# A two-layer hybrid decoder on one core: layer 1's down-projection without GpSimd, and the FFN's three-tap convolution accumulated in PSUM

## The chip, the cores and the metric

The kernel runs on one core of a Trainium2 chip. The metric is the device time of one execution in microseconds; the kernel before has a median of 2337.42 us over 3 runs. TensorE (PE) multiplies matrices into PSUM; VectorE (DVE), ScalarE (ACT) and GpSimd (POOL) do the element work; SyncE (SP) issues the transfers between HBM and SBUF.

## The reference, cut to what matters

The input is a sequence of 1024 positions of width 1024 in fp32. Two layers each have a mixer (layer 0: differential attention beside spatial gating; layer 1: a conformer convolution of width 31) and then a gated FFN with a causal convolution of width 3 over the positions. A final RMS norm ends it. The change lies in the FFN:

```
def conv_ffn(h, w_up, dw_w, dw_b, w_down):
    hh = causal_dwconv(h @ w_up, dw_w, dw_b)      # 2 * 2816 channels, 3 taps
    a, gate = jnp.split(hh, 2, axis=-1)
    return (a * jax.nn.silu(gate)) @ w_down       # 2816 -> 1024
```

## The kernel before, in words

Every fp32 operand of a matmul is split into a rounded high part and the rest: ACT casts the high part (L142), and DVE or POOL subtracts it to get the low part (L146). A product is then three passes (high by high, high by low, low by high).

**Up-projection.** `pair_steps` walks over 22 channel blocks j. For each j a gate block and a value block (128 channels each, 1024 positions) come from seven products of a Strassen-like scheme on half-size operands, 84 matmuls in all, in layers 0 and 1. ACT copies or DVE adds (L718, L720, L723) bring the products from PSUM into `row` tiles in SBUF. `conv` then makes the three taps of a row: ACT writes tap 2 and the bias into a tile `y` (L681), and DVE adds taps 1 and 0 with two SCALAR_TENSOR_TENSOR instructions over 1024 positions that read the row and `y` and write `y` (L683). The gate's `y` goes through Silu on ACT (L725), and DVE multiplies value by gate (L729). In layer 1, `finish` forms sums of two j's on POOL and DVE (L553 to L557) for the next stage and stores them to HBM in `phs`.

**Layer 1's down-projection.** `down_pair_steps` is again a seven-product scheme, with `ORDER` 2, 1, 5, 3, 6, 7, 4. Each product runs over 11 hidden pairs jj; product and jj make a unit of 12 matmuls (L819), so 77 units. A unit needs a weight quarter or a combination of quarters (`weight`, L781 to L787: products 5, 3, 6, 7 and 4 use combinations), its split, an activation block `ph` from `phs` and its split. Before the change POOL splits the weights, and POOL and DVE share the combinations. Quarters of the weight are loaded a product ahead of use; L771 is a DVE copy of one element, from the split activation of the unit before into the place that the load fills, which keeps the load behind that split. Product 2 accumulates in two single PSUM banks (`sbank`) and one double bank (`bank2`); there is one `bank2` buffer in the program. At the end of each product DVE adds the PSUM banks into the residual `xr` (L826), and the final norm follows.

**Order.** A scheduler simulates the program and orders each engine's instructions; a `pin` (new in the change) puts an instruction behind the one traced before it on its engine. The SP queue and each engine work strictly in their order.

Of the kernel before, what the change touches and what calls it, by code (L numbers as in the profile page):

```python
# [10 lines left out]
F32 = mybir.dt.float32  # L11
# [3 lines left out]
AF = mybir.ActivationFunctionType  # L15
# [33 lines left out]
HH = HT // 2  # L49
SLOT = {1: 0, 7: 1, 2: 2, 4: 3, 5: 4, 6: 5, 3: 6}  # L50
# [8 lines left out]
def trunk_kernel(ctx: ExitStack, tc: tile.TileContext, x, norm_mix_g, norm_ffn_g, ab_w_in, ab_w_out,  # L59
# [3 lines left out]
    nc = tc.nc  # L63
    x_in = x[0]
# [35 lines left out]
    def s4(shape, dt=F32):  # L100
        return wk.tile(shape, dt, tag="s4", name="s4", bufs=S4)

    def run(steps):
        for f in steps:
            f()
# [546 lines left out]
    def pair_steps(l, hT, T, js, up_pool):  # L652
# [26 lines left out]
        def conv(r, ct):  # L679
            y = s4([P, S])  # L680
            nc.scalar.activation(out=y, in_=r[:, 2:], func=AF.Identity, scale=dw[:, 2, ct:ct + 1], bias=dw[:, 3, ct:ct + 1])  # L681
            for k in (1, 0):
                nc.vector.scalar_tensor_tensor(out=y, in0=r[:, k:k + S], scalar=dw[:, k, ct:ct + 1], in1=y,  # L683
                                               op0=ALU.mult, op1=ALU.add)
            return y

        def f(j):
# [36 lines left out]
            yg = conv(rg, HT + j)  # L724
            nc.scalar.activation(out=yg, in_=yg, func=AF.Silu)  # L725
            product(A, 4, a4, False, True)
            nc.scalar.copy(out=rv_[:, 2:2 + CH], in_=A)
            yv = conv(rv_, j)
            nc.vector.tensor_tensor(out=yv, in0=yv, in1=yg, op=ALU.mult)  # L729
# [15 lines left out]
    def down_pair_steps(l, dpool):  # L745
# [20 lines left out]
        def load(n, jj, after=None):  # L766

            k, h = QUARTER[n]
            dst, r = W[jj][k][:, h * 512:(h + 1) * 512], (k * HH + jj) * P
            if after is not None:  # L770
                nc.vector.tensor_copy(out=dst[:, 0:1], in_=after)  # L771
            nc.sync.dma_start(out=dst, in_=w_dn[r:r + P, h * 512:(h + 1) * 512])

        def weight(n, jj):
# [8 lines left out]
            if n == 3:  # L783
                nc.gpsimd.tensor_sub(out=b12, in0=b22, in1=b12)
                nc.vector.tensor_add(out=b11, in0=b11, in1=b12)
            if n == 7:
                nc.gpsimd.tensor_sub(out=b21, in0=b21, in1=b11)  # L787
# [7 lines left out]
        def f(n, js):  # L795
# [14 lines left out]
            for i, jj in enumerate(js):  # L810
                us.append((unit(weight(n, jj), "pool"), unit(raw[:, i, :], "dve")))
                if n in (2, 1, 5):
                    load({2: 1, 1: 5, 5: 3}[n], jj, us[-1][1][:, 1, 0:1].bitcast(F32))
# [307 lines left out]
    with tc.tile_pool(name="down", bufs=1) as dpool:  # L1121
# [5 lines left out]
        for c in range(NCH):  # L1127
            x_from(xd[1])(c)
        run(ds[4:k])
# [38 lines left out]
```

## Time and profile before

| what | value |
|---|---|
| median of 3 runs (lowest to highest) | 2337.42 us (2334.6 to 2345.59) |
| profiled execution, its time and its span | 2339.52 us, 2337.6 us |
| PE busy | 2158.9 us, 92% of the span |
| DVE, ACT, POOL busy | 72%, 48%, 51% |
| layer 0 up-projection | 686 to 997 us and a little beyond |
| layer 1 up-projection | 1799 to 2087 us |
| layer 1 down-projection | 2081 to 2326 us, its start overlapped with the above |

The profiled execution lies 2.1 us above the median. A share of busy time is an average; what an engine waits for within a stage is in the rows further below.

### The profile page before, as it was taken

What the parts mean: (1) busy time and instruction counts of PE and PEld (TensorE: products, weight loads), DVE (VectorE), ACT (ScalarE), POOL (GpSimd) and SP (SyncE); (2) the same over time, 40 slices, a digit from 0 to 9 for tenths busy, and PEclk for the clock granted to TensorE, in tenths of its full rate; (3) what the DMA queues carried; (4) which work ended last, traced back from release to release, by engine and by line L of the source; (5) the groups of instructions that cost most, each with busy time, mean ns of one, the idle gap of its engine ahead of it and who ended that gap; (6) DMA issues with size and microseconds to landing.
All of it is one profiled execution on the core that took longest, in us unless ns stands there. A gap on an engine that the chain in (4) does not pass through costs nothing.

```text
span 2337.6 us, 28662 instructions
## 1 busy us (share of the span) xinstructions
PE 2158.9 (92%) x9882; PEld 1763.6 (75%) x9882; DVE 1675.2 (72%) x2721; ACT 1120.9 (48%) x1971; POOL 1198.4 (51%) x923
## 2 busy tenths in 40 slices
PE   8888879899999999999999879889898999989797
PEld 6677768788788888878887658767687877777586
DVE  6675747963976666655699969995685677767876
ACT  4344535743444444543556564655443444444254
POOL 3312311222644444545589827972565555656954
PEclk9999979999999999999999979989999999999999
DMA  7736545536422222465533513422643222257333
GB/s 236 214 104 194 175 151 176 161 95 204 130 91 88 88 82 82 138 207 196 172 117 117 171 55 101 143 77 87 215 140 122 88 93 100 86 204 240 102 117 99
DMA packets 299953, 318.81 MB, mean 136 GB/s; under 512 B 12444, under 2 KB 221600, under 8 KB 299296
## 3 DMA queue, kind: packets, MB, share of 16 engines
q1 hardware_dynamic: 293920, 302.30, 40.6%
q0 software_dynamic: 5888, 14.68, 2.1%
q8 instruction: 78, 1.28, 0.2%
q14 instruction: 67, 0.55, 0.1%
HBM read 253.76 MB, written 63.18 MB: 136 GB/s over the span
## 4 chain that ended last, share of the span: by engine, by line
PE 58%; DVE 23%; issue 7%; POOL 5%; ACT 5%; DMA 2%; SPq 0%; ACTq 0%; POOLq 0%; DVEq 0%
PE bank L675 15%; PE bank L304 14%; PE bank L267 11%; PE bank L856 6%; PE bank L819 5%; DVE sbank L1004 5%; DVE s L683 3%; DVE hl L146 3%; POOL hl L146 2%; DVE y L180 1%; POOL ap L1001 1%; ACT s L681 1%; PE sbank L464 1%; PE sbank L819 1%; ACT hl L142 1%
## 5 line engine op out<-in xcount | busy, mean ns | idle before, releaser
L146 POOL TENSOR_TENSOR hl<-raw,hl 128x512 fp32r<-128x512 f32 x456 | 671.7, 1491 | 510.4 <-ACT hl L142 486.4
L304 PE MATMUL bank<-big,hl 128*128 128x512 f32 x2112 | 500.8, 396 | 8.8 <-DVE big L223 2.7
L304 PEld LDWEIGHTS bank<-big,hl 128*128 128x128 f32 x2112 | 398.7, 191 | 95.1 <-ACT big L222 4.9
L142 ACT CAST hl<-raw 128x512 fp32r<-128x512 f32 x616 | 357.6, 617 | 228.5 <-PE bank L856 64.5
L267 PE MATMUL bank<-hl,big 128*128 128x512 f32 x1728 | 428.5, 402 | 20.8 <-POOL hl L146 9.8
L267 PEld LDWEIGHTS bank<-hl,big 128*128 128x128 f32 x1728 | 326.8, 193 | 91.9 <-POOL hl L146 10.4
L675 PE MATMUL bank<-big,hl 128*128 128x512 f32 x1440 | 346.9, 392 | 9.6 <-DVE row L720 8.2
L675 PEld LDWEIGHTS bank<-big,hl 128*128 128x128 f32 x1440 | 270.2, 189 | 72.0 <-DVE row L720 11.5
L683 DVE SCALAR_TENSOR_TENSOR s<-row,dw,s 128x1024 f32<-128x1024 f32 x120 | 198.1, 1651 | 123.3 <-ACT s L681 106.7
L675 PE MATMUL bank<-t,hl 128*128 128x512 f32 x1080 | 266.7, 396 | 6.9 <-ACT hl L142 6.9
L1004 DVE SCALAR_TENSOR_TENSOR sbank<-yb,cw,sbank 128x512 f32<-128x512 f32 x352 | 248.0, 747 | 6.0 <-ACT sbank L993 3.2
L856 PE MATMUL bank<-hl 128*128 128x512 f32 x1056 | 247.7, 392 | 4.3 <-DVE hl L146 3.9
L675 PEld LDWEIGHTS bank<-t,hl 128*128 128x128 f32 x1080 | 204.2, 190 | 53.9 <-ACT hl L142 8.0
L146 DVE TENSOR_TENSOR hl<-raw,hl 128x512 fp32r<-128x512 f32 x160 | 170.9, 1088 | 90.3 <-ACT hl L142 90.1
L856 PEld LDWEIGHTS bank<-hl 128*128 128x128 f32 x1056 | 196.2, 188 | 51.3 <-DVE hl L146 11.0
L819 PE MATMUL bank<-hl 128*128 128x512 f32 x726 | 176.4, 394 | 3.1 <-DVE xr L826 2.3
L1001 POOL TENSOR_TENSOR ap<-ap,pr 128x512 f32<-128x512 f32 x112 | 154.0, 1375 | 35.3 <-ACT ap L996 21.4
L819 PEld LDWEIGHTS bank<-hl 128*128 128x128 f32 x726 | 137.7, 190 | 33.9 <-DVE xr L826 2.7
L142 ACT CAST hl<-s 128x512 fp32r<-128x512 f32 x101 | 62.7, 621 | 163.0 <-DVE s L698 87.5
L146 DVE TENSOR_TENSOR hl<-ph,hl 128x512 fp32r<-128x512 f32 x72 | 101.9, 1428 | 44.8 <-ACT hl L142 44.8
L577 DVE SCALAR_TENSOR_TENSOR s<-bank,dw,s 128x510 f32<-128x510 f32 x112 | 83.4, 745 | 50.4 <-ACT s L574 49.0
L1000 ACT ACTIVATE pr<-yb,cw 128x512 f32<-128x512 f32 x112 | 80.8, 723 | 72.4 <-POOL ap L1001 72.1
(209 smaller groups left out, 2666.1 us busy)
## 6 DMA issues: line engine op xcount, KB each, us to landing
raw<-in_ffn_w_up SPq DMA_DIRECT2D x116, 512.0 KB, 4.3
raw<-in_ffn_w_down SPq DMA_DIRECT2D x44, 512.0 KB, 3.9
raw<-phd SPq DMA_DIRECT2D x44, 512.0 KB, 4.7
ph<-phs SPq DMA_DIRECT2D x33, 512.0 KB, 4.5
raw<-in_ab_w_in SPq DMA_DIRECT2D x64, 256.0 KB, 3.4
raw<-in_conv_w_in SPq DMA_DIRECT2D x32, 512.0 KB, 4.1
qd<-s SPq DMA_DIRECT2D x32, 256.0 KB, 2.9
qk<-qd POOLq DMA_DIRECT2D x8, 1024.0 KB, 7.3
```

What stands on the lines that cost most here:

```text
L142: nc.scalar.copy(out=hl_hi, in_=raw)
L146: eng.tensor_sub(out=hl_lo, in0=raw, in1=hl_hi.bitcast(F32))
L267: nc.tensor.matmul(ps, lhsT=hT[c][:, sa, d, tok(t)], rhs=units[d][:, sw, :], start=(n == 0), stop=(n == 3 * DT - 1))
L304: nc.tensor.matmul(ps, lhsT=hv[d // 4][:, sw, d % 4, :], rhs=hT[:, sa, d, :], start=(n == 0), stop=(n == 3 * DT - 1))
L577: nc.vector.scalar_tensor_tensor(out=y[:, sh:], in0=ps[:, :CH - sh], scalar=dw[:, k, ct:ct + 1], in1=y[:, sh:], op0=ALU.mult, op1=ALU.add)
L675: nc.tensor.matmul(ps, lhsT=hv[:, sw, d, :], rhs=B[n](sa, d), start=(start and i == 0), stop=(i == 11), skip_group_check=True)
L683: nc.vector.scalar_tensor_tensor(out=y, in0=r[:, k:k + S], scalar=dw[:, k, ct:ct + 1], in1=y, op0=ALU.mult, op1=ALU.add)
L819: nc.tensor.matmul(ps[k], lhsT=a[:, sa, k * P:(k + 1) * P], rhs=w[:, sw, :], start=(n in (5, 2, 1) and js[0] == 0 and i == 0), stop=(end a ...
L856: nc.tensor.matmul(ps, lhsT=phs[i][:, sa, k * P:(k + 1) * P], rhs=wds[i][:, sw, :], start=(dp == 0 and n == 0), stop=(dp == DP - 1 and n = ...
L1000: nc.scalar.activation(out=pr, in_=ys[ct][:, k:k + CH], func=AF.Copy, scale=cw[:, ct, k:k + 1])
L1001: nc.gpsimd.tensor_add(out=st["ap"], in0=st["ap"], in1=pr)
L1004: nc.vector.scalar_tensor_tensor(out=st["acc"], in0=ys[ct][:, k:k + CH], scalar=cw[:, ct, k:k + 1], in1=st["acc"], op0=ALU.mult, op1=ALU.add)
```

## The change

In `conv` the accumulator `y` becomes `bank2`, the one double bank of PSUM; Silu and the multiplication read it there and write SBUF tiles. In `down_pair_steps` all splits and combinations go to DVE, with the combinations pinned; the addition of b11 and b12 moves from product 3 to product 6; the one-element copies go; the loads are pinned on SP in the order of use, 5 units ahead of it, in place of behind a split; and the second half of the residual is loaded after 9 steps and not after 4.

```
+AHEAD = 5
+    pin = tc.keep_in_program_order
...
         def conv(r, ct):
-            y = s4([P, S])
+            y = bank2()
...
-            yg = conv(rg, HT + j)
-            nc.scalar.activation(out=yg, in_=yg, func=AF.Silu)
+            yg = s4([P, S])
+            nc.scalar.activation(out=yg, in_=conv(rg, HT + j), func=AF.Silu)
...
-            yv = conv(rv_, j)
-            nc.vector.tensor_tensor(out=yv, in0=yv, in1=yg, op=ALU.mult)
+            yv = s4([P, S])
+            nc.vector.tensor_tensor(out=yv, in0=conv(rv_, j), in1=yg, op=ALU.mult)
...
-            if after is not None:
-                nc.vector.tensor_copy(out=dst[:, 0:1], in_=after)
-            nc.sync.dma_start(out=dst, in_=w_dn[r:r + P, h * 512:(h + 1) * 512])
+            pin(nc.sync.dma_start(out=dst, in_=w_dn[r:r + P, h * 512:(h + 1) * 512]))
...
             if n == 3:
-                nc.gpsimd.tensor_sub(out=b12, in0=b22, in1=b12)
-                nc.vector.tensor_add(out=b11, in0=b11, in1=b12)
+                pin(nc.vector.tensor_sub(out=b12, in0=b22, in1=b12))
+            if n == 6:
+                pin(nc.vector.tensor_add(out=b11, in0=b11, in1=b12))
             if n == 7:
-                nc.gpsimd.tensor_sub(out=b21, in0=b21, in1=b11)
+                pin(nc.vector.tensor_sub(out=b21, in0=b21, in1=b11))
...
-                us.append((unit(weight(n, jj), "pool"), unit(raw[:, i, :], "dve")))
-                if n in (2, 1, 5):
-                    load({2: 1, 1: 5, 5: 3}[n], jj, us[-1][1][:, 1, 0:1].bitcast(F32))
+                us.append((unit(weight(n, jj), "dve"), unit(raw[:, i, :], "dve")))
+                p = ORDER.index(n) * HH + jj + AHEAD
+                if p // HH in (1, 2, 3):
+                    load(ORDER[p // HH], p % HH)
...
-        for c in range(NCH):
-            x_from(xd[1])(c)
-        run(ds[4:k])
+        x_from(xd[1])(0)
+        run(ds[4:9])
+        x_from(xd[1])(1)
+        run(ds[9:k])
```

From the lines 65 on the changed kernel's numbers are 2 higher (L683 is L685, L729 is L731, L146 is L148, L819 is L821, L826 is L828; L785 is L786 and L787 is L788). Up to the last j of layer 1 the order is the same on every engine, with `bank2` in place of an SBUF tile.

First PE, at the passage from the last j's seventh product (`big` weights, L675) to the down stage. The first name is the PSUM bank written, `hl` are split operands, of which each pair stands for one unit. Before:

```order
L675 MATMUL bank_17442<-big_13043,hl_17362 128x512 x12
L819 MATMUL sbank_17484<-hl_17491,hl_17494 128x512 x3
L819 MATMUL sbank_17485<-hl_17491,hl_17494 128x512 x3
L819 MATMUL bank2_17483<-hl_17491,hl_17494 128x512 x6
L675 MATMUL bank_17372<-big_14364,hl_17365 128x512 x12
L819 MATMUL sbank_17484<-hl_17515,hl_17518 128x512 x3
L819 MATMUL sbank_17485<-hl_17515,hl_17518 128x512 x3
L819 MATMUL bank2_17483<-hl_17515,hl_17518 128x512 x6
```

After the change, up to the same last product of the last j:

```order
L821 MATMUL sbank_17544<-hl_17551,hl_17554 128x512 x3
L821 MATMUL sbank_17545<-hl_17551,hl_17554 128x512 x3
L821 MATMUL sbank_17544<-hl_17573,hl_17576 128x512 x3
L821 MATMUL sbank_17545<-hl_17573,hl_17576 128x512 x3
L677 MATMUL bank_17430<-big_14396,hl_17423 128x512 x12
```

Behind it stand 12 single matmuls of units three and four on the two `sbank`s, and from the last of them on it reads:

```order
L821 MATMUL sbank_17545<-hl_17623,hl_17626 128x512
L821 MATMUL bank2_17543<-hl_17551,hl_17554 128x512 x6
L821 MATMUL bank2_17543<-hl_17573,hl_17576 128x512 x6
L821 MATMUL bank2_17543<-hl_17581,hl_17584 128x512 x6
L821 MATMUL bank2_17543<-hl_17623,hl_17626 128x512 x6
```

The `bank2` halves of the first four units now stand together behind the `sbank` halves of all four; before, each unit had both halves in a row.

Second DVE, at the same passage: the two convolutions of the last j (`row` tiles), the splits of the first units, and the sum L557. Before:

```order
L683 SCALAR_TENSOR_TENSOR s4_17456<-row_17368,dw1_440,s4_17456 128x1024
L771 COPY wb_17523<-hl_17528 128x1
L146 TENSOR_TENSOR hl_17572<-early_17486,hl_17572 128x512
L771 COPY wb_17523<-hl_17572 128x1
L146 TENSOR_TENSOR hl_17581<-early_17486,hl_17581 128x512
L771 COPY wb_17523<-hl_17581 128x1
L683 SCALAR_TENSOR_TENSOR s4_17474<-row_17370,dw1_440,s4_17474 128x1024 x2
L729 TENSOR_TENSOR s4_17474<-s4_17474,s4_17456 128x1024
L557 TENSOR_TENSOR s2_17562<-s4_17474,sx_17558 128x512
```

After the change, from the same convolution:

```order
L685 SCALAR_TENSOR_TENSOR bank2_17515<-row_17426,dw1_440,bank2_17515 128x1024
L148 TENSOR_TENSOR hl_17623<-wb_17579,hl_17623 128x512
L148 TENSOR_TENSOR hl_17626<-early_17546,hl_17626 128x512
L685 SCALAR_TENSOR_TENSOR bank2_17534<-row_17428,dw1_440,bank2_17534 128x1024 x2
L731 TENSOR_TENSOR s4_17533<-bank2_17534,s4_17514 128x1024
L148 TENSOR_TENSOR hl_17630<-wb_17579,hl_17630 128x512
L559 TENSOR_TENSOR s2_17616<-s4_17533,sx_17612 128x512
L148 TENSOR_TENSOR hl_17633<-early_17546,hl_17633 128x512
```

DVE now also splits the weights (`wb`), and the last multiplication L731 reads the `bank2` buffer that the down stage's first product takes next.

Third DVE, where product 3 gives way to product 6 (`w0` and `wb` are weight quarters). Before, the additions L785 of product 6 stand among the splits of product 5, for instance:

```order
L785 TENSOR_TENSOR w0_17512<-w0_17512 128x512
L771 COPY wb_17523<-hl_18037 128x1
L146 TENSOR_TENSOR hl_18073<-ph_18066,hl_18073 128x512
L781 TENSOR_TENSOR s2_18160<-wb_17621 128x512
L771 COPY wb_17523<-hl_18073 128x1
```

After the change they stand in product 6:

```order
L828 TENSOR_TENSOR xr_17702<-sbank_18026,xr_17702 128x512
L828 TENSOR_TENSOR xr_17702<-sbank_18027,xr_17702 128x512
L828 TENSOR_TENSOR xr_17702<-bank2_18025,xr_17702 128x512 x2
L786 TENSOR_TENSOR w0_17548<-w0_17548 128x512
L148 TENSOR_TENSOR hl_18509<-w0_17548,hl_18509 128x512
L148 TENSOR_TENSOR hl_18512<-ph_18506,hl_18512 128x512
L786 TENSOR_TENSOR w0_17570<-w0_17570 128x512
```

Each unit of product 6 is now an addition, the cast of its result on ACT, and two splits, in a row, behind the four residual additions that close product 3.

## Rows read from the trace of the kernel before

**Rows 1.** The page's chain of waits: shares of the span by line.

```profile
PE bank L675 15%; PE bank L304 14%; PE bank L267 11%; PE bank L856 6%; PE bank L819 5%; DVE sbank L1004 5%; DVE s L683 3%; DVE hl L146 3%; POOL hl L146 2%; DVE y L180 1%; POOL ap L1001 1%; ACT s L681 1%; PE sbank L464 1%; PE sbank L819 1%; ACT hl L142 1%
```

**Rows 2.** Stretches: busy (count) of PE, PEld, DVE, ACT, POOL; PE clock; DMA.

```profile
686.00:997.00 311.00, 310.87 (x1364) 255.05 (x1364) 206.50 (x215) 154.02 (x232) 153.60 (x130) 1.00 0.30 96
1799.00:2078.00 279.00, 268.37 (x1139) 215.60 (x1140) 200.59 (x181) 128.26 (x192) 163.47 (x126) 0.98 0.31 100
2081.00:2111.00 30.00, 21.90 (x90) 17.69 (x89) 20.17 (x22) 12.12 (x20) 17.55 (x11) 0.89 0.84 290
2111.00:2141.00 30.00, 30.00 (x134) 24.83 (x133) 22.57 (x32) 12.44 (x23) 16.70 (x12) 1.00 0.69 234
...
2171.00:2201.00 30.00, 22.45 (x77) 15.89 (x77) 27.81 (x25) 5.10 (x10) 30.00 (x20) 0.89 0.37 115
2201.00:2231.00 30.00, 27.70 (x116) 22.70 (x116) 17.13 (x14) 11.91 (x22) 23.23 (x16) 0.94 0.33 97
```

**Rows 3.** PE's waits in layer 1's up-projection: total us, times, longest.

```profile
PE bank L675 <- DVE row L720: 8.2, 5, 2.2
PE bank L675 <- ACT hl L142: 6.9, 3, 6.0
```

**Rows 4.** Chain of waits in layer 1's up-projection: start, us, what.

```profile
1859.02 1.91 DVE s L683
...
1913.91 2.00 DVE s L683
...
1916.51 1.65 DVE s L683
1918.68 1.69 DVE s L729
...
1922.29 1.59 DVE s L683
...
2067.48 1.92 DVE s L683
```

**Rows 5.** Single lines: count, duration ns min/median/max, first and last start.

```profile
L683 DVE SCALAR_TENSOR_TENSOR s<-row,dw,s x120: 1274/1554/2308, 707.7 to 2093.7; 128x1024 f32<-128x1024 f32 x120
L1004 DVE SCALAR_TENSOR_TENSOR sbank<-yb,cw,sbank x352: 730/746/757, 1162.7 to 1570.1; 128x512 f32<-128x512 f32 x176
L826 DVE TENSOR_TENSOR xr<-bank,xr x22: 665/678/692, 2122.9 to 2326.8; 128x512 f32<-128x512 f32 x22
L785 DVE TENSOR_TENSOR wb<-wb x8: 1437/1745/1775, 2170.2 to 2197.1; 128x512 f32<-128x512 f32 x8
```

**Rows 6.** PE's waits from 2081 to 2327 us.

```profile
PE sbank L819 <- POOL hl L146: 9.8, 8, 3.7
PE sbank L819 <- ACT hl L142: 8.1, 1, 8.1
PE bank L819 <- DVE xr L826: 2.3, 1, 2.3
```

**Rows 7.** Timeline of PE: start, us, what, [idle before, releaser].

```profile
2083.91 2.88 PE L675 MATMUL bank<-big,hl 128*128 128x512 f32 x12
2086.63 1.52 PE L819 MATMUL sbank<-hl 128*128 128x512 f32 x6
...
2105.77 2.07 PE L819 MATMUL sbank<-hl 128*128 128x512 f32 x4 [8.10 <-ACT hl L142]
```

**Rows 8.** Timelines of DVE (first three) and ACT: start, us, what, [idle, releaser].

```profile
1861.45 1.72 DVE L683 SCALAR_TENSOR_TENSOR s<-row,dw,s 128x1024 f32<-128x1024 f32 x1
...
2091.57 0.69 DVE L146 TENSOR_TENSOR hl<-early,hl 128x512 fp32r<-128x512 f32 x1
...
2095.91 1.23 DVE L729 TENSOR_TENSOR s<-s,s 128x1024 f32<-128x1024 f32 x1
...
2089.78 1.06 ACT L725 ACTIVATE s<-s 128x1024 f32<-128x1024 f32 x1 [1.70 <-DVE s L683]
...
2091.88 0.60 ACT L142 CAST hl<-wb 128x512 fp32r<-128x512 f32 x1
```

More of the change, by code (lines that the diff above doesn't have):

```diff
@@ L764, in place, with load @@
                 W[jj] = [W["big"][:, i, :], W["big"][:, i + 1, :]]
-        def load(n, jj, after=None):
+        def load(n, jj):
             k, h = QUARTER[n]
             dst, r = W[jj][k][:, h * 512:(h + 1) * 512], (k * HH + jj) * P
-            if after is not None:
-                nc.vector.tensor_copy(out=dst[:, 0:1], in_=after)
-            nc.sync.dma_start(out=dst, in_=w_dn[r:r + P, h * 512:(h + 1) * 512])
+            pin(nc.sync.dma_start(out=dst, in_=w_dn[r:r + P, h * 512:(h + 1) * 512]))
         def weight(n, jj):
```

## The prediction

> **What bounds the kernel now.** I read the page's chain of waits first, then busy time by stretch, then in each stretch that the change touches PE's waits, and at last the chain and the timeline where PE waits. The chain ends mostly on PE: L675, the up-projection's matmuls, is its largest share, and L683, the taps that the change touches, has 3% [rows 1]. Busy time by stretch says where PE is not full [rows 2]. In layer 0's up-projection PE is busy 310.87 of 311.00 us at clock 1.00: nothing that DVE does there is worth time. In layer 1's it is busy 268.37 of 279.00 us. In the down stage the slices differ: 134 matmuls in 30 us from 2111 us, but 90 from 2081 us, 77 from 2171 us and 116 from 2201 us, at clocks of 0.89, 0.89 and 0.94. Full pace is one unit of 12 matmuls in 2.72 us, the distance of the two starts 2083.91 and 2086.63 [rows 7], so 0.2267 us a matmul and 132.3 in 30 us. The three slices lose 9.6, 12.5 and 3.7 us by that; another 4 us lies scattered over the rest.
>
> In layer 1's up-projection PE's waits name DVE's additions out of PSUM (8.2 us) and one cast at the entry (6.9) [rows 3]. The chain shows what makes those additions late: a loop through DVE, ACT and POOL. The same L683 comes back at 1859.02, and for the fifth time after that at 2067.48 [rows 4]: 208.46 us over five turns, 41.7 us for two j's. Their 168 matmuls need 38.1 us. PE loses 3.6 us a turn, 18 us in five; before the first turn it is fed.
>
> **The taps in PSUM.** L683 lasts 1274 ns at least, 1554 at the median and 2308 at most; the spread goes with GpSimd's work beside it. An instruction of the same kind whose accumulator is in PSUM, L1004, spans 730 to 757 ns over all its 352 executions, with GpSimd's taps running beside it; L826, which reads one operand from PSUM, 665 to 692 [rows 5]. L685 becomes such an instruction at twice the length. L1004's 747 ns are 214 ns plus 512 elements at 0.96 per ns (the pace that 746 and 1274 ns for 512 and 1024 elements agree with, within 7 ns); 1024 elements give 1.28 us, and L683's own undisturbed minimum is the same 1.27. The upper bound is two L1004, 1.49. I take 1.28, since nothing in the 352 rows ever rose.
>
> On the chain of one turn stand L683 with 1.91, 2.00, 1.65 and 1.59 us [rows 4], and one of 1.72 [rows 8], which the chain writes as issue. At 1.28 each they save 0.63, 0.72, 0.37, 0.31 and 0.44, 2.5 in all. L729 at 1.69 falls to 1.21 to 1.25 (two L826, or its own undisturbed 1.23 [rows 8]), 0.45. ACT writes PSUM instead of SBUF at four places; I allow 0.05 us each (unknown; 0.1 at most, from either sign), 0.2 against. The turn becomes 41.7 - 2.5 - 0.45 + 0.2 = 39.0 us, still above PE's 38.1. Five turns give 13.5 us; the last j, 0.5 more: **14 us**, between 5 (L685 at 1.49, when only the contended ones gain) and 18 (PE never waits). What the chain has besides, the contended SBUF operations L695 to L698 and the three sums on POOL, stays.
>
> [...]
>
> One buffer for all accumulators is the other side of the change. Each j now runs ACT tap, two taps on DVE, Silu, and then the same with the multiplication: 1.24 + 2.56 + 1.06 and 1.24 + 2.56 + 1.23, 9.9 us of holding in 19.5 us. The buffer adds a wait only where the previous reader (L725 on ACT, L729 on DVE) is not done when the next L681 could start. ACT does L725 ahead of the value row's L681 in its own order already [rows 8], and the work that covers the other handing over is the next j's products. I put it at nothing, with 1 us a turn as the bound, 5 us.
>
> Layer 0: nothing in PE's 311 us; its last conv, before the down stage, ends earlier by at most 2 us. I take 1.
>
> **The down stage, its first units.** Before, PE does four units at the passage and stands 8.10 us until 2105.77, for a cast of a `ph` block [rows 7, 6], then four matmuls take 2.07 us where full pace is 0.91: the 9.6 us of the first slice, at a mean clock of 0.89. After, the four units' `bank2` halves wait for the last conv. The last product of the last j ends at a time t (2086.6 before). Then follow the copy out, Silu, and taps of the value row: L681 to t + 4.3, two taps to t + 6.9, L731 to t + 8.15, from the durations above. PE has 12 `sbank` matmuls for that, 2.72 us: it stands 5.4 us, and about 2 us go to the lower clock behind it, 7.5 to 8. Behind that stand 24 matmuls, 5.4 us, in which the `ph` splits of the next units must come: L559 waits on POOL's sums until about t + 12 (three of 1.3 us) and DVE's splits behind it cost 0.69 each [rows 8], two a unit, while PE needs 2.72. The SP queue asks for the first residual half and three weights before the first `ph`; at 290 GB/s [rows 2] that lands before PE wants it by some 2 us. So 9.6 becomes 7.5 to 8: gain **2 us**, between -4 (`ph` late) and +4.
>
> **The middle of the stage.** PE waited 9.8 us in eight places for POOL's low parts [rows 6], in the slice where POOL was busy 30.00 of 30.00 us [rows 2] and L785 took 1.75 us beside it [rows 5]; clock and knock-on make it 12.5 + 2.8. After, GpSimd has nothing to do there, so each DVE operation takes its undisturbed 0.69 us (L146 at 2091.57 [rows 8]). A unit of products 5, 3 and 7 needs a combination and two splits, 2.07 us, less than PE's 2.72; products 2 and 1 need 1.38. In product 6 the addition, the cast on ACT and the splits follow each other: 0.69 + 0.62 + 0.05 or so for the two hand-overs + 0.69 + 0.69 = 2.74, if the cast is not covered, the one place near PE's pace; DVE's own back-to-back rate of 0.60 brings it to 2.57. Loads no longer wait for splits; five units ahead are 13.6 us, against some 4 us to land. The 15.3 us become 1: gain **14**, between 9 and 15. At the boundary of products 3 and 6 PE waited 2.3 us for L826 and lost 3.7 with the clock; now four L828 (2.7) and the first unit of product 6 stand there in a row, 2.25 to 2.8 us: gain 0.5 (-1 to 2). The final norm beside the last products now shares DVE with splits: -0.5 (-3 to 0).
>
> **The sum.** 14 + 1 + 2 + 14 + 0.5 - 0.5 = 31 us. From the profiled 2339.5 us that is 2308.5; the median is 2.1 us under the profiled execution, so 2306. The likeliest's own range is 2299 to 2314.
>
> **Rivals.**
> 1. Only half arrives. Either L685 takes 1.49 us or another link sets the loop (the three POOL sums, 3.9 us a turn, or the SBUF operations beside them), so layer 1's loop gives 5 and not 14; or the product 6 chain runs at 3.0 us, 11 x 0.28 = 3, and `ph` comes late by 4. Gain 14 to 22, 2316 to 2324. For it: the rest of the loop is untouched. Against: the rows of L1004.
> 2. No change to measure. The taps' gain is taken by the single buffer (5) and the front (-4 in place of +2), and the middle gives 9 where PE merely waits elsewhere: 5 - 5 - 4 + 9 = 5, so 2332.
> 3. Slower: DVE cannot carry the down stage. The point from which it decides is 2.72 / 3 = 0.907 us an operation. If splits into the rounded format kept the 1.4 us that they often take beside GpSimd, units with a combination would take 4.2 us and the 33 of products 5, 3 and 6 alone would lose 33 x 1.5 = 49 us: net of the 15 us won elsewhere and the 15 of old waits, 19 us slower, 2356. Against it: splits of 0.69 us in rows where POOL is idle [rows 8], and POOL has no work left there but three sums and the norm.
> 4. More arrives: PE never waits in layer 1's loop, front at its best: 37 us, 2300.
>
> **How the numbers follow.** Forecast 0.66, half 0.17, no change 0.07, slower 0.06, more 0.04. The range must leave out no more than 2 in 10: forecast, more, and most of half, 2296 to 2324. About 0.5%, 12 us, is what a measurement of this kernel can tell from no change; faster by more than that are forecast, half and more, 0.87, from which I take 0.02 for halves that fall short: 0.85. Same 0.09, slower 0.06.
>
> **What would show it.** L685 at 1.28 us with minimum and maximum close together; the turn in layer 1's loop at 39 us, still on DVE and ACT, and PE's waits there at some 5 us; PE's stand at the first units 5 to 6 us, now for L731 and not for a `ph` cast; no waits for POOL in the down stage, DVE at 0.6 to 0.7 us a split, and PE at 130 matmuls or more in 30 us from product 1 to product 7. Wrong would be a longer L685, PE waits on `hl` in product 6, or a `ph` or weight transfer as the releaser in the middle.

## The result, and the profile after

The changed kernel takes 2305.7 us (median of 4 runs, 2301.7 to 2310.99), the kernel before 2336.39 us beside it: a ratio of 0.9862, 95% interval 0.9829 to 0.9895, so 31 us faster. Forecast were 2306 us. The profiled execution has a span of 2303.9 us, 33.7 less than before; of that some 4 us lie ahead of layer 1's up-projection (its matmuls resume after the entry wait at 1795.33 us and not 1799.31), 3.0 of them before layer 0's up-projection begins, where nothing was changed. The sum came out right, but not all of its terms did: that it fits to a microsecond is luck, as the part on the prediction shows.

Stretches of the changed kernel, columns as in [rows 2]: layer 0's up-projection, layer 1's, then six of the slices of 30 us from the passage to the down stage on.

```profile
682.70:993.70 311.00, 310.87 (x1366) 255.16 (x1365) 184.49 (x215) 154.24 (x233) 129.86 (x130) 1.00 0.30 96
1836.00:2042.00 206.00, 206.00 (x905) 169.52 (x904) 144.86 (x145) 99.23 (x147) 107.09 (x99) 1.00 0.31 102
...
2054.00:2084.00 30.00, 25.10 (x99) 19.41 (x99) 20.87 (x26) 13.43 (x20) 3.79 (x3) 0.89 0.61 217
2084.00:2114.00 30.00, 30.00 (x134) 24.86 (x133) 19.63 (x32) 12.47 (x22) 0.00 (x0) 1.00 1.03 390
...
2144.00:2174.00 30.00, 29.45 (x130) 24.09 (x129) 20.55 (x34) 12.44 (x22) 0.00 (x0) 1.00 0.40 119
2174.00:2204.00 30.00, 26.59 (x104) 21.04 (x103) 17.11 (x27) 7.98 (x14) 0.00 (x0) 0.89 0.28 86
...
2234.00:2264.00 30.00, 28.06 (x123) 22.59 (x122) 27.46 (x73) 18.22 (x35) 3.43 (x3) 1.00 0.52 167
```

Layer 0 was full and is full. Layer 1's loop, which had lost PE time in every turn, is now full too: 206.00 of 206.00 us. In the down stage three slices lose against 132.3 matmuls: the passage 7.5 us (99), the boundary of products 3 and 6 6.4 us (104), product 7 with the final norm 2.1 us (123). The middle of the stage is full but for 0.5 us (130 of 132.3), with GpSimd at nothing.

What PE waits for in the changed kernel from 2054 us on, the three largest: total us, times, longest.

```profile
PE bank L821 <- DVE s L731: 4.4, 1, 4.4
PE bank L821 <- ACT hl L144: 3.8, 3, 2.6
PE bank L821 <- DVE v L173: 1.5, 1, 1.5
```

No wait for GpSimd is left [rows 6]; the wait for a `ph` cast at the passage has become one for the last multiplication, as forecast.

### The profile page after: what moved, and what is told of

Same layout as the page of the kernel before. It is cut to its first block, busy times and chain, and to the rows that moved or that the text cites. A ratio compares the mean times of both kernels' runs of the same rounds, so it can differ in the third digit from the quotient of the medians.

```text
span 2303.9 us, 28559 instructions
## 1 busy us (share of the span) xinstructions
PE 2147.5 (93%) x9882; PEld 1760.4 (76%) x9882; DVE 1601.8 (70%) x2787; ACT 1120.9 (49%) x1971; POOL 1002.2 (43%) x824
## 3 DMA queue, kind: packets, MB, share of 16 engines
q8 instruction: 78, 1.28, 0.2%
## 4 chain that ended last, share of the span: by engine, by line
PE 70%; DVE 18%; issue 4%; DMA 3%; ACT 3%; POOL 3%; SPq 0%; ACTq 0%; DVEq 0%; POOLq 0%
PE bank L677 25%; PE bank L306 14%; PE bank L269 11%; PE bank L821 7%; PE bank L858 6%; DVE sbank L1006 5%; DVE hl L148 2%; PE sbank L821 2%; DVE y L182 1%; POOL ap L1003 1%; PE sbank L466 1%; POOL hl L148 1%; DVE xn L197 1%; PE sbank L213 1%; ACT hl L144 1%
## 5 line engine op out<-in xcount | busy, mean ns | idle before, releaser
L148 POOL TENSOR_TENSOR hl<-raw,hl 128x512 fp32r<-128x512 f32 x456 | 632.0, 1404 | 506.4 <-ACT hl L144 479.5
L685 DVE SCALAR_TENSOR_TENSOR bank<-row,dw,bank 128x1024 f32<-128x1024 f32 x120 | 154.5, 1287 | 140.6 <-ACT bank L683 138.1
L148 DVE TENSOR_TENSOR hl<-raw,hl 128x512 fp32r<-128x512 f32 x160 | 169.6, 1080 | 93.1 <-ACT hl L144 92.8
L821 PE MATMUL bank<-hl 128*128 128x512 f32 x726 | 176.8, 398 | 10.4 <-DVE s L731 4.4
L821 PEld LDWEIGHTS bank<-hl 128*128 128x128 f32 x726 | 139.4, 193 | 42.3 <-issue 5.8
L1003 POOL TENSOR_TENSOR ap<-ap,pr 128x512 f32<-128x512 f32 x112 | 153.8, 1373 | 34.5 <-ACT ap L998 20.7
L1112 POOL TENSOR_TENSOR xr<-xr,gain 128x512 f32<-128x512 f32 x10 | 14.5, 1479 | 202.3 <-ACT xn L1104 176.8
```

The source lines that it names most:

```text
L148: eng.tensor_sub(out=hl_lo, in0=raw, in1=hl_hi.bitcast(F32))
L821: nc.tensor.matmul(ps[k], lhsT=a[:, sa, k * P:(k + 1) * P], rhs=w[:, sw, :], start=(n in (5, 2, 1) and js[0] == 0 and i == 0), stop=(end a ...
L1003: nc.gpsimd.tensor_add(out=st["ap"], in0=st["ap"], in1=pr)
```

## The experiments

All times are medians with the kernel before run on the same chip. To see where a difference lies I read two lengths from each trace: "up", from where layer 1's up-projection resumes after its entry wait to the start of the last j's last matmul, and "down", from there to the start of the last matmul of the down stage. What follows, 13 to 14 us, is alike in all.

| kernel | us | before | ratio | 95% interval | up | down |
|---|---|---|---|---|---|---|
| before | | 2336.39 | | | 287.1 | 238.0 |
| changed | 2305.7 | 2336.39 | 0.9862 | 0.9829 to 0.9895 | 269.7 | 225.7 |
| e1 convolution only | 2319.93 | 2344.42 | 0.9898 | 0.9885 to 0.9912 | 268.3 | 237.8 |
| e2 down stage only | 2325.03 | 2344.42 | 0.9926 | 0.9913 to 0.9939 | 287.1 | 222.5 |
| e3 second tap to SBUF | 2303.45 | 2344.42 | 0.9829 | 0.9815 to 0.9842 | 271.1 | 219.8 |
| e4 weight splits on GpSimd | 2319.91 | 2344.42 | 0.9899 | 0.9884 to 0.9914 | 271.1 | 236.7 |
| e5 three additions ahead | 2302.3 | 2338.3 | 0.9848 | 0.9829 to 0.9866 | 271.0 | 218.8 |
| e6 last convolution in SBUF | 2309.57 | 2338.3 | 0.9875 | 0.986 to 0.989 | 271.2 | 223.3 |
| e7 norm off GpSimd | 2305.71 | 2338.3 | 0.9862 | 0.9848 to 0.9877 | 270.9 | 223.1 |
| e8 all three | 2303.64 | 2338.3 | 0.9851 | 0.9835 to 0.9868 | 271.1 | 220.2 |
| e9 e5 + e6, second half later | 2297.99 | 2339.83 | 0.9831 | 0.9813 to 0.9848 | 270.9 | 216.4 |
| e10 residual halves together | 2312.72 | 2339.83 | 0.9889 | 0.9872 to 0.9905 | 270.7 | 227.6 |
| e11 e3 + e5 | 2300.59 | 2339.83 | 0.9835 | 0.982 to 0.9851 | 271.1 | 217.1 |
| e12 changed, again | 2306.99 | 2339.83 | 0.9865 | 0.9847 to 0.9884 | 270.8 | 225.3 |

"Down" split by product, in us: the first column runs from the start of the last j's last matmul to the end of product 2, the others from the start of a product's first matmul to that of the next product's. Full pace is 29.9 us a product. Products 1 and 4, the second and the last, take 29.7 to 29.9 in every run.

| kernel | end of 2 | 5 | 3 | 6 | 7 |
|---|---|---|---|---|---|
| before | 37.3 | 45.4 | 34.1 | 29.9 | 31.6 |
| changed | 35.2 | 29.9 | 34.7 | 33.8 | 32.6 |
| e12 changed, again | 36.0 | 29.9 | 34.7 | 32.9 | 32.1 |
| e1 | 36.2 | 46.3 | 34.2 | 29.9 | 31.6 |
| e2 | 35.6 | 29.9 | 34.7 | 32.0 | 30.6 |
| e3 | 33.0 | 29.9 | 34.7 | 31.9 | 30.6 |
| e4 | 36.1 | 30.1 | 34.9 | 36.6 | 39.5 |
| e5 | 34.2 | 29.9 | 30.8 | 31.5 | 32.9 |
| e6 | 36.4 | 29.9 | 34.7 | 32.0 | 30.6 |
| e7 | 36.0 | 29.9 | 34.7 | 32.9 | 30.0 |
| e8 | 38.4 | 29.9 | 30.8 | 31.5 | 30.0 |
| e9 | 32.6 | 29.9 | 30.8 | 31.5 | 32.0 |
| e10 | 35.9 | 29.9 | 34.7 | 32.9 | 34.5 |
| e11 | 33.2 | 29.9 | 30.8 | 31.5 | 32.0 |

The two traces of one and the same changed kernel differ by 0.8 to 0.9 us in two of the columns; differences of that size mean nothing.

**The two halves apart.** e1 is the kernel before with the three edits of `conv`, Silu and the multiplication; e2 is the changed kernel with those three undone.

> The convolution in PSUM alone; the down stage as before. Theory (each half pays in its own stage): layer 1's up-projection, from its first matmul after the entry wait to the end of the last j's last product, takes 270 us as in the changed kernel (287.5 before), PE has no wait on DVE additions there, and the total gain over before is 17 to 20 us, less what the bank2 wait costs at the passage: the old down stage keeps its waits for GpSimd's low parts (about 10 us). So 2317 to 2321. Rival (the two halves need each other, since the old down stage takes bank2 for its first unit too): the first units stand 4 to 8 us longer than before and 2322 to 2328 remains. A turn of two j's is 38 to 39 us in both.

> The down stage without GpSimd and with loads in order alone; the convolution accumulates in SBUF as before. Theory: a turn of two j's stays at 41.7 us and L685's counterpart at 1.27 to 2.31 us; the down stage from the end of the last product to the last matmul takes 225 to 227 us (238 before, 226 with both), or some 3 less since bank2 is free at its start: the total is 2320 to 2326. Rival (GpSimd leaving the stage is worth nothing without the shorter passage): 2332 or more.

Each half pays in its own stage: e1's up is short and its down is that of before, e2 the other way round. (In e1 half a unit stands ahead of the last j's last product and not a whole one, which takes 1.4 us from its up and adds them to its down.) The stand that e1's rival expected at the first units is not there: they end no later than before. In e1 the old down stage meets the slice that it had before [rows 2], with GpSimd busy without a gap:

```profile
2147.00:2177.00 30.00, 22.09 (x73) 15.54 (x71) 29.13 (x25) 5.70 (x10) 30.00 (x19) 0.83 0.42 131
```

By these lengths the halves add up but for 3 us: e2's down is 222.5, the changed kernel's 225.7. (By the medians they gain 24.5 and 19.4 us on a chip whose kernel before is 5 to 8 us slower than elsewhere and on which the changed kernel wasn't run; the sum can't be read from those.) The 3 us are not a price of `bank2` at the passage: at the end of product 2 the two are level, 35.6 and 35.2 us, and the difference lies in products 6 and 7, to which the part on the final norm returns. With the accumulators in SBUF, e2 has a wait of 5.2 us at the passage for a cast instead, as the kernel before had [rows 7]:

```profile
2106.25 1.22 PE L821 MATMUL sbank<-hl 128*128 128x512 f32 x2 [5.19 <-ACT hl L144]
```

**Which operand makes a tap long.** In e3 the second tap reads PSUM and writes SBUF:

```
             y = bank2()
...
+            z = s4([P, S])
             for k in (1, 0):
-                nc.vector.scalar_tensor_tensor(out=y, in0=r[:, k:k + S], scalar=..., in1=y, ...)
+                nc.vector.scalar_tensor_tensor(out=y if k else z, in0=r[:, k:k + S], scalar=..., in1=y, ...)
-            return y
+            return z
```

Silu and the multiplication then work on `z` in SBUF.

> As the changed kernel, but the second tap reads the accumulator in PSUM and writes an SBUF tile, which Silu and the multiplication read. Theory (a second SBUF input is what GpSimd's work lengthens, the place of the output is not): both taps stay at 1.27 to 1.30 us, all 120 of them; the multiplication, which again reads two SBUF tiles, goes back to 1.2 to 1.7 us; the time stays within 3 us of the changed kernel, 2303 to 2309, as PE is the bound in the loop. Rival (an accumulator kept in PSUM on both sides is needed): half of the taps go to 1.6 us in the mean with a maximum over 2 us, the turn goes up by about 1 us, and the time to 2309 to 2314.

The taps of the changed kernel, of e3 (L686, one row for each output) and e3's multiplication: count, ns min/median/max, first and last start. First the changed kernel:

```profile
L685 DVE SCALAR_TENSOR_TENSOR bank<-row,dw,bank x120: 1277/1290/1292, 704.6 to 2070.9; 128x1024 f32<-128x1024 f32 x120
```

and e3:

```profile
L686 DVE SCALAR_TENSOR_TENSOR bank<-row,dw,bank x60: 1278/1289/1291, 707.0 to 2073.9; 128x1024 f32<-128x1024 f32 x60
L686 DVE SCALAR_TENSOR_TENSOR s<-row,dw,bank x60: 1268/1280/1282, 708.3 to 2075.2; 128x1024 f32<-128x1024 f32 x60
L732 DVE TENSOR_TENSOR s<-s,s x30: 1212/1220/2308, 716.5 to 2076.5; 128x1024 f32<-128x1024 f32 x30
```

With GpSimd at work beside them, e3's taps take 1278 to 1291 ns with their output in PSUM and 1268 to 1282 ns with it in SBUF: where the output goes makes 10 ns here at most. One input in PSUM was enough to keep every tap under 1.3 us, and the multiplication, which reads two SBUF tiles again, has its 2308 ns maximum back, against 1282 ns at most for the taps that write SBUF. e3 also hands `bank2` over one multiplication earlier: PE waits 2.9 us at the passage and not 4.4. Down is 219.8 us, 5.4 to 5.9 shorter than in the changed kernel's two profiles, of which the passage gives 2.2 to 3.0 and products 6 and 7 the rest. The median is 2 us below the changed kernel's, within what was expected. By the ratio, 0.9829, e3 would be the faster, but its interval overlaps with the changed kernel's, and it is from the chip with the slow kernel before: e11, which has e3's edit and one more that shortens down by another 2.7 us, has 0.9835 on another chip. That e3 beats the changed kernel is not shown by the times.

**GpSimd's place in the down stage.** e4 gives the weights' splits back, with the combinations on DVE and the loads in order:

```
-                us.append((unit(weight(n, jj), "dve"), unit(raw[:, i, :], "dve")))
+                us.append((unit(weight(n, jj), "pool"), unit(raw[:, i, :], "dve")))
```

> As the changed kernel, but the weights' low parts in the down stage are again subtracted on GpSimd; combinations stay on DVE and loads in program order. Theory (GpSimd's presence in the stage makes the waits): DVE's splits and combinations rise from 0.69 to 1.2 to 1.75 us while GpSimd splits, each low part on GpSimd takes 1.3 to 2.2 us, and in products 5, 3 and 6 a unit costs more than 2.72 us: PE waits for low parts return, 8 to 15 us in all, total 2312 to 2322. Rival (the loads in order were the gain, DVE's room is not needed): the time stays at 2304 to 2308 and PE waits for GpSimd are under 3 us.

The time is as the theory has it, 11 us of the down stage's gain gone, but not the place. Slices of e4:

```profile
2118.00:2148.00 30.00, 30.00 (x135) 24.82 (x134) 26.14 (x26) 13.27 (x25) 17.24 (x13) 1.00 0.57 193
2148.00:2178.00 30.00, 29.41 (x129) 23.67 (x127) 20.45 (x19) 11.50 (x22) 14.92 (x11) 1.00 0.43 132
...
2238.00:2268.00 30.00, 23.26 (x92) 17.77 (x91) 29.67 (x61) 16.77 (x35) 20.72 (x13) 0.94 0.42 133
```

Products 5 and 3 keep PE full although GpSimd splits and DVE's `ph` splits take 1.37 us beside it. What is lost lies in products 6 and 7. In product 6 a unit's addition, casts and splits follow each other; two additions stand 3.23 us apart, over PE's 2.72:

```profile
2198.69 0.68 DVE L786 TENSOR_TENSOR w<-w 128x512 f32<-128x512 f32 x1
2200.65 1.34 DVE L148 TENSOR_TENSOR hl<-ph,hl 128x512 fp32r<-128x512 f32 x1 [1.28 <-ACT hl L144]
2201.92 0.68 DVE L786 TENSOR_TENSOR w<-w 128x512 f32<-128x512 f32 x1
```

In the changed kernel they stand 2.66 us apart (2192.76, 2195.41, 2198.07). In the slice of product 7 PE loses 9.1 us, where GpSimd does splits and the norm's multiplications at once.

**The boundary of products 3 and 6.** The changed kernel loses 6.4 us there. PE first, then DVE:

```profile
2190.44 1.67 PE L821 MATMUL bank<-hl 128*128 128x512 f32 x6 [0.79 <-DVE xr L828]
2194.74 9.53 PE L821 MATMUL bank<-hl 128*128 128x512 f32 x28 [2.63 <-ACT hl L144]
```

```profile
2192.15 0.69 DVE L828 TENSOR_TENSOR xr<-bank,xr 128x512 f32<-128x512 f32 x1 [1.76 <-PE bank L821]
2192.76 0.68 DVE L786 TENSOR_TENSOR w<-w 128x512 f32<-128x512 f32 x1
2194.20 0.69 DVE L148 TENSOR_TENSOR hl<-w,hl 128x512 fp32r<-128x512 f32 x1 [0.76 <-ACT hl L144]
```

The fourth residual addition waits for product 3's last matmul, and product 6's first addition stands behind it in DVE's queue, though its operands have long been there. e5 makes the first three ahead:

```
-            if n == 6:
+            if n == 6 and jj > 2:
                 pin(nc.vector.tensor_add(out=b11, in0=b11, in1=b12))
...
+            if n == 3 and end:
+                for jj in (0, 1, 2):
+                    b11, b12 = W[jj][0][:, :512], W[jj][0][:, 512:]
+                    pin(nc.vector.tensor_add(out=b11, in0=b11, in1=b12))
```

> As the changed kernel, but product 6's first three additions of b11 and b12 (jj 0 to 2) are made at the end of product 3, ahead of the residual additions. Theory (the stand at the boundary of products 3 and 6 is the chain of L828, addition, cast and split behind the residual additions): PE's wait of 2.6 us for ACT's cast goes, the stretch of 30 us that holds the boundary gets back some 5 of the 6.4 us that it loses (104 matmuls before), and the down stage is 4 to 5 us shorter; the ratio to the kernel before is 0.002 lower. Rival (PE waits there for the residual additions to free banks, or the additions only move the wait into product 3's last units): the loss stays above 4 us.

The slice that holds the boundary is full in e5:

```profile
2176.00:2206.00 30.00, 30.00 (x135) 24.82 (x134) 20.59 (x33) 10.28 (x18) 0.00 (x0) 1.00 0.31 94
```

Down is 218.8 us, 6.4 to 6.9 under the changed kernel's two profiles; products 3 and 6 together lose 6.2 us less than in the first of them. The measured ratio is 0.0014 lower, within the intervals: the gain is seen in the trace. The longest wait in product 7 grew from 1.5 to 2.5 us.

**The passage.** e6 frees `bank2` before the down stage:

```
-        def conv(r, ct):
-            y = bank2()
+        def conv(r, ct, y):
...
+            last = l == 1 and j == js[-1]
-            nc.scalar.activation(out=yg, in_=conv(rg, HT + j), func=AF.Silu)
+            nc.scalar.activation(out=yg, in_=conv(rg, HT + j, yg if last else bank2()), func=AF.Silu)
...
-            nc.vector.tensor_tensor(out=yv, in0=conv(rv_, j), in1=yg, op=ALU.mult)
+            nc.vector.tensor_tensor(out=yv, in0=conv(rv_, j, yv if last else bank2()), in1=yg, op=ALU.mult)
```

> As the changed kernel, but the last j of layer 1 accumulates its two convolutions in SBUF tiles, so that bank2 is free when the down stage begins. Theory (the 4.4 us wait at the first units is for bank2 alone): no wait for the last multiplication is left, PE goes on through the first four or five units, then stands at most 2 to 3 us for a ph cast or a weight; the first units are 3 to 6 us shorter. Rival (the ph and weight transfers are as late as in the kernel before, bank2 only covers it): PE stands 4 to 8 us for a cast of a ph block instead and nothing is won.

The theory fell here: the wait for the multiplication is gone and a longer one stands in its place. PE, SP's queue and the chain of waits of e6, in this order:

```profile
2085.70 1.22 PE L821 MATMUL sbank<-hl 128*128 128x512 f32 x2 [7.16 <-ACT hl L144]
```

```profile
2073.85 0.38 SPq L869 DMA_DIRECT2D xr<-xd  x1
2075.05 0.33 SPq L809 DMA_DIRECT2D ph<-phs  x1
```

```profile
2075.42 9.01 DMA wb<-in_ffn_w_down
```

The scheduler, with its order changed, put the 2 MB of the residual's second half ahead of the first `ph` and its weight, which then took 9.0 us to land: it is this weight's cast that PE waits for. e6's down is still 2.4 us shorter than the changed kernel's first, but that is in products 6 and 7; its passage is no shorter (36.4 us to the end of product 2), as the rival has it. e9 tells this from a `ph` that is late by its own issue: it pins that load behind the loads traced before it (and has e5's additions).

```
-            nc.sync.dma_start(out=xr[c], in_=src[c * CH:(c + 1) * CH, :].rearrange(...))
+            i = nc.sync.dma_start(out=xr[c], in_=src[c * CH:(c + 1) * CH, :].rearrange(...))
+            if src is xd[1] and c == 1:
+                pin(i)
```

> As the changed kernel with the last j's convolutions in SBUF and three additions ahead, and with the load of the residual's second half pinned on SP behind the loads traced before it, so that it isn't put ahead of the first ph block. Theory (in the run with the last convolution in SBUF alone, the 7.2 us stand was for that 2 MB transfer ahead of the first ph block, whose own issue waits for the last tap): the first ph and its weight land 4 to 5 us after issue, PE stands 2 to 4 us at the sixth unit, and the passage is 3 to 5 us shorter than in the changed kernel; the ratio to the kernel before is 0.980 to 0.984. Rival (the first ph block is late by its own issue, which waits for the last tap, whatever stands ahead of it): PE still stands 5 us or more, and the ratio is that of the run with three additions ahead alone, 0.985.

In e9 the same weight lands in 5.0 us and PE stands 3.4 us. First the chain of waits, from the last tap on, then PE:

```profile
2074.14 1.21 DVE s L684
...
2075.40 0.33 SPq L809
...
2075.77 4.96 DMA wb<-in_ffn_w_down
```

```profile
2081.99 1.22 PE L825 MATMUL sbank<-hl 128*128 128x512 f32 x2 [3.40 <-ACT hl L144]
```

The passage is 2.6 to 3.4 us shorter than in the changed kernel's two profiles. So both were true in part: 3.8 us of the 7.2 were the 2 MB ahead, 3.4 us remain because the first `ph` is asked for only once the last tap is done (2075.40), and the weight stands behind it in SP's queue. That the `ph` tile lies where a `row` tile lay would explain why it is asked for so late; it was not tried.

**The final norm.** e7 has `eng = nc.vector` for all of L1112.

> As the changed kernel, but the final norm's multiplications by the gain (L1112) are on VectorE and not on GpSimd. Theory (the splits of 1.78 us around 2231 to 2237 us are long because GpSimd multiplies beside them): no split in the down stage is over 0.8 us, PE's wait of 1.5 us and its loss of 2.1 us in product 7 fall to under 1, and the time is 1 to 3 us lower. Rival (the waits there come from the norm's small instructions in DVE's queue): the wait in product 7 stays or grows by the ten multiplications of 0.69 us, and the time is the same or up to 3 us higher.

In the changed kernel, GpSimd's multiplications and DVE beside them:

```profile
2229.72 6.41 POOL L1112 TENSOR_TENSOR xr<-xr,gain 128x512 f32<-128x512 f32 x4 [100.05 <-ACT xn L1104]
```

```profile
2231.50 1.78 DVE L148 TENSOR_TENSOR hl<-wb,hl 128x512 fp32r<-128x512 f32 x1
```

In e7 no split in the stage is over 0.76 us and the wait of 1.5 us is gone; down is 223.1, 2.1 to 2.6 us shorter, beside e12 all of it in product 7. The ratio, 0.9862, doesn't show it: the mechanism is seen in the trace, a gain in the time is not.

The long splits alone don't make PE wait, though. e3 has the same four multiplications on GpSimd and the same long splits beside them, and PE goes through product 7 with no stand but 0.2 us ahead of it; GpSimd, DVE and PE of e3:

```profile
2230.84 6.43 POOL L1113 TENSOR_TENSOR xr<-xr,gain 128x512 f32<-128x512 f32 x4 [98.68 <-ACT xn L1105]
2236.03 1.79 DVE L148 TENSOR_TENSOR hl<-wb,hl 128x512 fp32r<-128x512 f32 x1
2229.15 30.20 PE L822 MATMUL bank<-hl 128*128 128x512 f32 x132 [0.20 <-DVE xr L829]
```

The changed kernel, at the same place:

```profile
2242.82 19.36 PE L821 MATMUL bank<-hl 128*128 128x512 f32 x84 [1.48 <-DVE v L173]
```

What differs is the order that the scheduler gave DVE there. In the changed kernel, e5, e9, e10, e11 and e12 DVE does combinations and the norm's small instructions for 7.1 to 7.2 us without a split (2234.98 to 2242.08 in the changed kernel), and product 7 takes 32.0 to 34.5 us; in e2, e3 and e6 the longest such stretch is 2.6 to 3.0 us, and it takes 30.6. So GpSimd's multiplications do not make the loss alone, and the 3 us between e2 and the changed kernel come from product 7, the stand ahead of it (0.7 to 1.2 us against 0.2) and product 6's 132 matmuls behind product 3, which take 33.10 us in the changed kernel, at a granted clock of 0.68 in the mean from 2194.7 to 2204.3 us, and 31.82 in e6, whose product 6 is as long as e2's. e7 shortened that stretch as well (4.1 us); what the order would cost without GpSimd, no run shows.

**Together.** e8 has e5, e6 and e7; e11 has e3 and e5; e10 asks for both residual halves together again; e12 is the changed kernel once more.

> The changed kernel with all three: three additions ahead, the last convolution in SBUF, the norm's multiplications on VectorE. Theory (three separate stands in one stage, each paid once): the gains add up, 8 to 12 us below the changed kernel, a ratio of 0.981 to 0.983 to the kernel before, and PE's waits in the down stage are under 4 us. Rival (one stand covers the next): under 5 us below the changed kernel.

> As the changed kernel, but both halves of the residual are asked for together after 4 steps, as in the kernel before. The scheduler leaves the second half behind the weights and ph blocks of the first units even so, some ten transfers earlier than in the changed kernel. Theory (the place of that half matters only ahead of the first ph block): PE's waits in the first units stay at 4 to 5 us, for the last multiplication, and the time is within 3 us of the changed kernel. Rival (2 MB anywhere in the first 30 us delays weights): a new wait of 2 to 5 us for a cast of a weight or ph behind a transfer.

> The changed kernel with the second tap written to SBUF and three additions ahead. Theory (the first frees bank2 a multiplication earlier, 1.2 us and its clock; the second takes out the stand at products 3 and 6): PE's wait for bank2 is 2.9 us, no wait of 2.6 us at the boundary, waits in the down stage 6 to 7 us in all, and the time is 4 to 8 us below the changed kernel of the same chip. Rival (what the boundary gives comes back at product 7): under 3 us below.

> The changed kernel itself, on the same chip as the other three, to compare them with. Both theories: a ratio of 0.985 to 0.988 to the kernel before, and the waits of its first profile: 4.4 us for the last multiplication at the first units, 2.6 us for a cast between products 3 and 6.

e8 fell short by the same 2 MB: PE stands 8.1 us at the passage, and its down of 220.2 is longer than e5's alone. e9 and e11, which shorten the passage (32.6 and 33.2 us to the end of product 2) and the boundary, have the shortest down stages and ratios of 0.9831 and 0.9835 beside 0.9865 for the changed kernel on the same chip: medians 9.0 and 6.4 us lower. The intervals of e9 and e12 just meet, at 0.9847 and 0.9848, and those of e11 and e12 overlap; the down stages, 8.8 and 8.2 us shorter, say the same from the traces: both are faster than the changed kernel, e11 by a margin that the times alone don't secure. In e10 the wait at the passage is the same 4.4 us, and no wait for a transfer shows; its median is 5.7 us above e12's, its interval overlaps with e12's. Its down is 2.3 us longer, all in product 7, far behind that load; up to the end of product 6 the two traces agree within 0.1 us. So the trace is for the theory; the time lies outside the 3 us that it allowed, and nothing in the trace ties that to the load.

## Why the prediction was right, by its steps

**The taps in PSUM: mechanism and price right, the size a little small.** L685 was forecast at 1.28 us and takes 1.277 to 1.292, with no long ones. ACT's taps into PSUM, for which 0.05 us each, an allowance that no row gives, was set against, take 1.210 us in the mean of layer 1's loop where the kernel before has 1.244 into SBUF: a small gain instead. The single `bank2` cost nothing in the loop. The turn was forecast at 39.0 us with DVE and ACT still ahead of PE; it is 38.35: the same L685 starts at

```profile
1967.21 1.29 DVE L685 SCALAR_TENSOR_TENSOR bank<-row,dw,bank 128x1024 f32<-128x1024 f32 x1 [0.50 <-ACT bank L683]
...
2043.90 1.29 DVE L685 SCALAR_TENSOR_TENSOR bank<-row,dw,bank 128x1024 f32<-128x1024 f32 x1 [0.50 <-ACT bank L683]
```

two turns apart. So PE bounds it and the term is 17.4 us (287.1 to 269.7), not 14, near the bound of 18. The step that was too small is "the contended SBUF operations L695 to L698 and the three sums on POOL, stays": those operations got shorter as well, for instance, before and after, in 206 us each:

```profile
L695 DVE TENSOR_TENSOR s<-raw 128x512 f32<-128x512 f32 x10 | 12.3, 1231 | 0.0
```

```profile
L697 DVE TENSOR_TENSOR s<-raw 128x512 f32<-128x512 f32 x11 | 12.6, 1150 | 0.0
```

L697 and L698 of before (L699 and L700 after) went from 1181 to 1135 ns and from 1176 to 1135. Two of each in a turn and the splits beside them make some 0.5 us, an estimate from these means, and ACT's taps, shorter where 0.2 us a turn was set against, another 0.3: that brings the 39.0 close to PE's own 38.1. Why they got shorter is seen on the other side, in GpSimd's splits in this loop, before, after, and in e1, which has the convolution alone:

```profile
L146 POOL TENSOR_TENSOR hl<-raw,hl 128x512 fp32r<-128x512 f32 x41 | 76.4, 1880 | 5.2 <-ACT hl L142 5.2
```

```profile
L148 POOL TENSOR_TENSOR hl<-raw,hl 128x512 fp32r<-128x512 f32 x40 | 57.7, 1459 | 7.1 <-ACT hl L144 7.0
```

```profile
L146 POOL TENSOR_TENSOR hl<-raw,hl 128x512 fp32r<-128x512 f32 x40 | 57.7, 1458 | 7.1 <-ACT hl L142 7.0
```

e2, with the convolution as before, has 1894 ns. From 1880 to 1459 ns, the 40 splits of five turns are some 17 us less of GpSimd beside DVE; that this is what shortened DVE's operations is argued, not shown by a run of its own. A tap in PSUM is not much longer than an undisturbed one in SBUF: the median in PSUM is 1290 ns, the minimum in SBUF was 1274 [rows 5], 16 ns less, and e3's taps into SBUF take 1280.

**Layer 0: 1 forecast, some 2.4 in the traces.** PE was full in the up-projection and stayed so. At the start of its down stage the kernel before waits for a split:

```profile
PE bank L856 <- DVE hl L146: 1.7, 1, 1.7
```

The same wait is in e2, and not in the changed kernel or e1, where the convolution is in PSUM. From its first matmul to its last that stage takes 346.7 us before and 347.8 in e2, 344.3 in the changed kernel and 344.4 in e1.

**The passage: right, with 7.5 us lost of 7.5 to 8.** 4.9 us of standing (4.4 for the multiplication, 0.5 for a split) were forecast as 5.4, the rest is the lower clock behind it, a granted clock of 0.71 in the mean from 2073.6 to 2081.4 us: 24 matmuls took 7.77 us instead of 5.4.

```profile
2073.60 7.77 PE L821 MATMUL bank<-hl 128*128 128x512 f32 x24 [4.37 <-DVE s L731]
```

The forecast had `ph` land 2 us before it is wanted, behind the first residual half and three weights in the queue; that it is asked for only after the last tap (at 2072.26 us here) was not in it. The stand for `bank2` covered that: e9 shows PE standing 3.4 us for the weight behind that `ph` once `bank2` is free.

**The middle: 14 forecast, 15.5 found, for another reason in part.** The 15.5 us are product 5's alone, 45.4 us before and 29.9 after. The reason given, undisturbed DVE operations of 0.69 us, is what the trace shows, but e4 shows that products 5 and 3 did not need it. Before, GpSimd had a split and up to two combinations a unit, each 1.7 us and so 5 us against PE's 2.72; it was the bound, at 30.00 of 30.00 us [rows 2], and DVE, with 27.81, nearly as full. In places three combinations stood between two of GpSimd's splits:

```profile
2174.77 1.75 POOL L784 TENSOR_TENSOR wb<-wb 128x512 f32<-128x512 f32 x1
2176.48 3.40 POOL L787 TENSOR_TENSOR wb<-wb 128x512 f32<-128x512 f32 x2
2179.85 1.71 POOL L146 TENSOR_TENSOR hl<-s,hl 128x512 fp32r<-128x512 f32 x1
```

To take the combinations off it, with the loads in order, was enough there. The undisturbed 0.69 us are needed in product 6, where e4 takes 36.6 us and the changed kernel 32.9 to 33.8; in product 7, where e4 loses the other 7 us, GpSimd's multiplications and the order of DVE's queue play a part as well. What of the middle is the combinations' and what the loads' order, no run tells apart.

**The boundary of products 3 and 6: wrong, by 3 to 5 us.** Forecast was a gain of 0.5 (-1 to 2); the slice loses 6.4 us where the one of before lost 3.7, and products 3 and 6 together take 4.4 us more than before (3.6 in e12). The step "four L828 and the first unit of product 6 stand there in a row, 2.25 to 2.8 us" priced the 2.63 us wait well, but left out the 0.79 us before it and the lower clock behind it, 0.68 in the mean from 2194.7 to 2204.3 us, where 28 matmuls take 9.53 us and not 6.35; before, the first addition of product 6 had been made long ahead. e5, in which both products together take 62.2 us where the changed kernel has 68.4 and full pace is 59.8, shows that this is most of it.

**Product 6 and the norm.** Forecast were 2.57 to 2.74 us a unit against 2.72; it is 2.66 and PE doesn't wait within the product, as close a call as it looked. The norm was forecast at -0.5 for sharing DVE; product 7 takes 32.6 us (32.1 in e12) where it took 31.6, so 0.5 to 1.0 us, within the range given. The cause is not DVE's sharing alone: e7 shows that GpSimd's four multiplications make DVE's splits 1.78 us long (0.76 at most without them), and e3 that these cost little where the norm's small instructions stand between splits.

In sum 17.4 us in the up-projection, 2.4 in layer 0 and 12.3 in the down stage (passage 2.1, middle 15.5, boundary -4.4, norm -1.0) stand against 14, 1 and 16: errors of up to 5 us with opposite signs. The mechanisms were right in the main; that the sum lands within a microsecond of the measured 2305.7 is luck.

## What to carry to other kernels

Beside a busy GpSimd, try one input of a long VectorE instruction in PSUM: here the taps, up to 2308 ns long before, took 1292 at most, and GpSimd's own splits became shorter as well (1880 to 1459 ns in the mean), which a sum over VectorE alone leaves out. When work leaves an overloaded engine, ask which of its instructions made the overload and which can stay: the trace of the kernel before shows only that the engine is full. An operation that is moved later in an engine's queue takes its place behind whatever waits there (here product 6's first addition, behind a residual addition before which DVE stood 1.76 us), and a big load can take the place of a small one that is waited for (here a weight that landed in 9.0 us and not 5.0); look at both at each boundary, and pin them. Where a scheduler orders the engines, an edit in one stage can reorder another: compare two traces stage by stage before a difference is put down to the edit (here 3 us in products 6 and 7 that no edit there made).

## What the runs showed of the hardware that had not been expected

GpSimd's instructions were longer beside VectorE's taps in SBUF: with the taps accumulated in PSUM, GpSimd's 128x512 splits in the same loop went from 1880 to 1459 ns in the mean, and to 1458 in e1, where nothing else was changed. A tap with its accumulator in PSUM and its output in SBUF (median 1280 ns) is as fast as one that stays in PSUM (1289 ns). A 256 KB weight load landed 5.0 us after its issue, and 9.0 us after it with 2 MB asked for just ahead of it on the same queue.
